# Two-layer trunk of delta-rule and linear-attention heads: another order of the stages, and head outputs read back in parts

## The chip, the cores and the metric

The kernel runs on one core of one Trainium2 chip. The metric is the time of one execution on the device in microseconds (us). Engines are named as in the profile: PE is TensorE, DVE is VectorE, ACT is ScalarE, POOL is GpSimd, SP is SyncE. All DMA transfers of this kernel are issued by SP.

## The reference

One sequence of 2048 tokens with 1024 channels passes two layers. Each layer projects its input to 3608 columns, runs four Gated DeltaNet heads (a short convolution on q, k and v, a delta-rule recurrence over chunks) beside four GLA heads (a gated linear attention over chunks), normalises each head, multiplies it by a SiLU gate, mixes the eight heads with one output projection, and ends with a residual LayerNorm. Everything is float32.

```python
def gated_delta_rule_chunked(q, k, v, g, beta):
    """S_t = a_t (I - b_t k_t k_t^T) S_{t-1} + b_t k_t v_t^T,  o_t = S_t^T q_t."""
    ...
    lower = jnp.eye(c, dtype=f32) + jnp.where(strict, kk * decay, 0.0)
    rhs = jnp.concatenate([vc * bc[..., None], k_beta * jnp.exp(G)[..., None]], axis=-1)
    uw = lax.linalg.triangular_solve(lower, rhs, left_side=True, lower=True)
    ...

def gla_chunked(q, k, v, gk):
    """S_t = diag(exp(gk_t)) S_{t-1} + k_t v_t^T,  o_t = S_t^T q_t."""
    ...

def hybrid_layer(x, w_in, conv_w, ...):
    proj = jnp.einsum("btd,de->bte", x, w_in)
    (dn_q, dn_k, dn_v, dn_z, dn_b, dn_a, g_q, g_k, g_v, g_z, g_r) = _split(proj, IN_SIZES)
    dn_qkv = jax.nn.silu(causal_short_conv(jnp.concatenate([dn_q, dn_k, dn_v], axis=-1), conv_w))
    ...
    o_dn = gated_delta_rule_chunked(q, k, v, g, beta)
    o_dn = head_rms_norm(o_dn, dn_norm_g) * jax.nn.silu(dn_z.reshape(...))
    ...
    o_gla = gla_chunked(gq, gk, gv, log_f)
    o_gla = head_rms_norm(o_gla, gla_norm_g) * jax.nn.silu(g_z.reshape(...))
    o = jnp.concatenate([o_dn.reshape(bsz, t, DN_WIDTH), o_gla.reshape(bsz, t, GLA_WIDTH)], axis=-1)
    y = jnp.einsum("bte,ed->btd", o, w_out)
    return layer_norm(DEEPNORM_ALPHA * x + y, ln_g, ln_b)
```

## The kernel before

**Halves, blocks, chunks.** A layer is computed in two halves of 1024 tokens; the program thus has four halves, and the state of the recurrences is carried from one to the next. A half has two blocks of 512 tokens (b0, b1), and a block has four chunks of 128 (c0 to c7 over the half). Heads 0 to 3 of the output are the delta-rule heads, heads 4 to 7 the GLA heads, which are handled in two pairs (p0, p1).

**Precision.** Matmuls of the projections run in a reduced float32 format; every operand is split in a high part (tiles `wh`, `xt`) and a low part (`wl`, and a second `xt`), and a product takes three matmuls per 128 rows of weights. `load_group` loads 128 columns of the input weights (`wr`) and splits them: a cast to `wh` on ACT, a subtraction to `wl`. `proj_group` multiplies them with a block of the input into a bank `pj` of PSUM: 24 matmuls of 128x512. There are two `pj` banks, three `tr`, two `ch` and one `mg`.

**Stages of a half.** `dense_qk(p)` projects q and k of a GLA pair; `g1(p, b)` is the short-range part of GLA (many matmuls of 128x32 and 64x64), `g2(p, b)` the long-range part, which ends in `finish_head` (four transposes and a copy). `keys(h)`, `values` and `queries` project and convolve a delta-rule head; `dn_decay` spreads its decay factors by way of HBM (`decd`). `dn_invert(h)` inverts the triangular systems of a head, seven steps on DVE, and `dn_merge(h)` joins the inverted blocks with small matmuls in bank `mg`. `gates(e)` projects the gate of head e, multiplies the head's output by it and writes the result, transposed, to HBM: `og[b][e]`.

**The recurrence.** `dn_rec(h, b)` goes through the four chunks of a block. Per chunk it has five matmuls in two `ch` banks: state by keys (its result goes through DVE to `rr`), state by queries (scaled to `qs`), the inverted block by `rr` (scaled on DVE to `vn`), and two products with `vn`, of which one updates the state `Sd` on DVE. Each step waits for the one before: PE, DVE, PE, DVE, PE, DVE.

**Output projection.** `split_o(c, og)` reads the eight gated heads of a chunk back from HBM (512 KB into a tile `m`), casts them to a `wh` tile and subtracts to a `wl` tile. `out_half` multiplies with one half of the columns of the output weights, which `load_wo` has put in `xt` tiles: 16 matmuls with the high part, head by head, then 8 with the low part. `out_proj` runs the 16 pairs of chunk and column half in a fixed sequence, c0, c1 and c2 with the first column half first.

**What sets the order.** No engine gets its instructions as they are written. A `Recorder` notes every operation of the program, with what it reads and writes. `order()` (line 231) then builds the order of each engine by going through a model of time: of the operations whose inputs are done and for whose tile a slot is free (`SLOTS`, `BANKS`), an engine takes the one that was recorded first (`key = program position − lift`), looking at later ones where that one can't start. The durations in it are estimates of the planner. The operations are then issued in this order, each engine in order. So the sequence of the stages in the source is a sequence of priorities, and any change to it can move operations on all engines. Since the recorder's helper issues everything, all lines of the profile read L428, and groups are told apart by tile names.

The stages stand in the source in this sequence (before): dense_qk(0), g1(0,0), values of the second GLA pair, g2(0,0), g1(0,1), dn_decay 0 and 1, dense_qk(1), g2(0,1), dn_decay 2 and 3, g1(1,0), gates 4 and 5, g2(1,0), keys(0), dn_invert(0), g1(1,1), g2(1,1), values and queries of head 0 as one stage (`vq`), dn_merge(0), gates 6 and 7, keys(1); then for each head h the recurrence over both blocks, dn_invert(h+1), vq(h+1), dn_merge(h+1), keys(h+2), and gates(0) after head 2. The gates of heads 1 to 3 follow the recurrence, block 0 first.

## Time and profile before

| | before |
|---|---|
| time, median of 3 runs | 2248.61 us (2245.91 to 2249.0) |
| the profiled execution | 2245.92 us, span 2244.2 us |
| busy PE, DVE, ACT, POOL | 97%, 66%, 49%, 23% of the span |
| DMA | 215.32 MB, 96 GB/s over the span |
| mean granted clock of PE | 0.990 |

PE is the tensor engine's matmuls, PEld its weight loads, which overlap with them. A float32 matmul that isn't in the reduced format shows as two records. Matmul records begin before their forerunner ends, so the time from one start to the next is what one costs. In brackets behind a row of the timeline stands how long the engine sat idle before it, and which engine and tile released it; rows of waits give the total, how often, and the longest. "PEclk" is the share of full clock that PE was granted; in the rows of windows it is the third number from the end.

### The profile page before, as it was taken

The page shows a single profiled execution, that of the slowest core. Times are in us where ns is not written, and L with a number is a line of the kernel's source. Part 1 is how long each engine was busy: PE and PEld are TensorE (multiplying, and loading weights), DVE is VectorE, ACT ScalarE, POOL GpSimd, SP SyncE. Part 2 cuts the span into 40 slices and gives each one's busy share as a digit, 9 for nine tenths or more (in the row PEclk, how much of TensorE's full clock was granted, in tenths as well). Part 3 has the DMA queues.
Part 4 walks back from the last instruction along what each step waited for, and adds up shares of the span by engine and source line. Part 5 has one row for each costly group of instructions (what it writes and reads, how often), then busy time and mean ns, then how long its engine had stood idle before and what let it go on. Part 6 is the DMA issues. An engine that isn't in the chain of part 4 may idle for free.

```text
span 2244.2 us, 44454 instructions
## 1 busy us (share of the span) xinstructions
PE 2165.7 (97%) x16914; PEld 1798.9 (80%) x16914; DVE 1485.1 (66%) x3444; ACT 1098.9 (49%) x3123; POOL 523.8 (23%) x880
## 2 busy tenths in 40 slices
PE   8999999999999999999999999999999999999998
PEld 7877777878887777787888777778788877877877
DVE  3547688756454768875645586887564458688756
ACT  4665455431466545543146654554215665455420
POOL 3333122101143213210122421320011242132001
PEclk9999999999999999999999999999999999999999
DMA  4242222373224131236322323223732232222361
GB/s 139 62 110 64 76 56 58 100 228 123 86 58 123 51 99 45 61 108 215 128 72 71 110 60 92 60 59 106 225 116 69 79 93 66 86 60 69 104 192 57
DMA packets 264542, 215.32 MB, mean 96 GB/s; under 512 B 53060, under 2 KB 211080, under 8 KB 264328
## 3 DMA queue, kind: packets, MB, share of 16 engines
q1 hardware_dynamic: 264328, 212.48, 32.0%
q8 instruction: 133, 2.18, 0.4%
q14 instruction: 81, 0.66, 0.1%
HBM read 166.23 MB, written 46.20 MB: 95 GB/s over the span
## 4 chain that ended last, share of the span: by engine, by line
PE 79%; DVE 10%; DMA 5%; ACT 4%; issue 2%; SPq 0%; POOL 0%; DVEq 0%; ACTq 0%; POOLq 0%
PE pj L428 60%; PE ch L428 9%; PE tr L428 7%; DVE tmp L428 2%; DVE R L428 2%; DMA ud<-Tb 2%; PE mg L428 2%; DVE m L428 2%; ACT m L428 2%; DVE kq L428 1%; DMA U<-ud 1%; DMA m<-nd 1%; DVE Tb L428 1%; ACT wh L428 1%; DMA nd<-T 1%
## 5 line engine op out<-in xcount | busy, mean ns | idle before, releaser
L428 PE MATMUL pj<-xt,wh 128*128 128x512 f32 x4096 | 1102.4, 407 | 18.8 <-ACT wh L428 10.4
L428 PEld LDWEIGHTS pj<-xt,wh 128*128 128x128 f32 x4096 | 748.6, 191 | 167.4 <-ACT wh L428 12.1
L428 PE MATMUL pj<-xt,wl 128*128 128x512 f32 x2048 | 556.6, 401 | 0.0
L428 PEld LDWEIGHTS pj<-xt,wl 128*128 128x128 f32 x2048 | 372.7, 188 | 70.2 <-issue 0.9
L428 POOL TENSOR_TENSOR s<-s,mhalf 128x4 f32<-128x4 f32 (+2 forms) x80 | 94.8, 1185 | 537.2 <-DVE s L428 532.8
L428 POOL TENSOR_TENSOR wl<-wr,wh 128x512 fp32r<-128x512 f32 (+2 forms) x94 | 135.2, 1446 | 308.8 <-ACT wh L428 238.5
L428 PE MATMUL pj<-wh,xt 128*128 128x256 f32 (+1 forms) x1024 | 197.6, 290 | 0.0
L428 DVE TENSOR_TENSOR m<-m,m 128x256 f32<-128x256 f32 (+1 forms) x272 | 132.3, 499 | 55.2 <-ACT m L428 48.8
L428 PEld LDWEIGHTS pj<-wh,xt 128*128 128x128 f32 x1024 | 162.1, 190 | 0.8 <-ACT xt L428 0.4
L428 ACT CAST wh<-wr 128x1024 fp32r<-128x1024 f32 (+2 forms) x116 | 118.2, 1022 | 76.7 <-PE pj L428 57.5
L428 DVE SCALAR_TENSOR_TENSOR kq<-raw,cw,kq 128x512 f32<-128x512 f32 x192 | 152.9, 803 | 3.9
L428 PE MATMUL pj<-wl,xt 128*128 128x280 f32 (+1 forms) x512 | 131.7, 290 | 0.0
L428 DVE TENSOR_TENSOR wl<-wr,wh 128x512 fp32r<-128x512 f32 (+3 forms) x118 | 88.4, 769 | 61.9 <-ACT wh L428 60.9
L428 DVE SCALAR_TENSOR_TENSOR m<-m,pj 128x512 f32<-128x512 f32 x64 | 43.8, 685 | 114.6 <-PE pj L428 114.6
L428 ACT CAST wh<-m 128x1024 fp32r<-128x1024 f32 x32 | 33.1, 1046 | 158.3 <-PE pj L428 158.3
L428 ACT ACTIVATE sq<-m 128x128 bf16<-128x128 f32 x128 | 39.5, 308 | 140.9 <-DVE m L428 132.0
L428 PEld LDWEIGHTS ch<-Sd,kq 128*128 128x128 f32 x512 | 79.9, 192 | 25.6 <-DVE Sd L428 14.2
L428 DVE COPY m<-pj 128x256 f32<-128x256 f32 x18 | 7.6, 423 | 137.0 <-PE pj L428 137.0
L428 PEld LDWEIGHTS pj<-wl,xt 128*128 128x128 f32 x512 | 97.5, 191 | 0.1
L428 PEld LDWEIGHTS ch<-vn,m 128*128 128x128 f32 x512 | 72.8, 192 | 26.9 <-DVE vn L428 17.3
L428 PE MATMUL ch<-Sd,kq 128*128 128x128 f32 x512 | 88.3, 281 | 5.4 <-DVE Sd L428 5.4
L428 PE MATMUL ch<-vn,m 128*128 128x128 f32 x512 | 83.0, 282 | 9.5 <-DVE vn L428 9.5
(192 smaller groups left out, 3420.0 us busy)
## 6 DMA issues: line engine op xcount, KB each, us to landing
wr<-in_w_in_dram SPq DMA_DIRECT2D x104, 512.0 KB, 4.4
m<-decd SPq DMA_DIRECT2D x64, 256.0 KB, 4.3
og<-m SPq DMA_DIRECT2D x64, 256.0 KB, 4.0
m<-in_w_out_dram SPq DMA_DIRECT2D x32, 512.0 KB, 6.0
m<-og SPq DMA_DIRECT2D x32, 512.0 KB, 6.0
m<-in_x_dram SPq DMA_DIRECT2D x16, 512.0 KB, 5.6
m<-gr SPq DMA_DIRECT2D x32, 256.0 KB, 6.1
decd<-m SPq DMA_DIRECT2D x32, 256.0 KB, 2.2
```

Source lines behind the costliest of these rows:

```text
L428: getattr(getattr(self.nc, o.eng), o.name)(*[real(a) for a in o.args], **{k: real(a) for k, a in o.kw.items()})
```

## The change

The sequence of the stages is written as a string, `PLAN`, and differs from the sequence above:

- dense_qk(1) now comes ahead of dense_qk(0);
- g2(p,b) follows its g1(p,b) sooner, and the values of the second GLA pair come after both blocks of the first;
- values and queries of a head are two stages (`v`, `y`), and each block of the recurrence is one (`r` with head and block), with other stages between the two blocks of head 0 (`r00`, `r01`);
- gates 6 and 7 move from ahead of the recurrence to behind the second block of head 0, gates(0) between the queries and the values of head 3.

`split_o` takes a list of parts. For chunks 0, 1 and 2, heads 4 to 7 are read, cast and subtracted first, then heads 0 to 2, then head 3; the other chunks are read whole. `out_half` goes through the heads in the order 4 to 7, 0 to 3. The products and sums are the same; only the order in which the eight heads are summed differs. Per half there are six more DMA transfers, six more casts and six more subtractions.

```diff
--- before.py
+++ after.py
@@ -548,6 +548,10 @@
          "s1": 16, "Sc": 3, "nd": 2, "ud": 2, "og0": 2, "og1": 2, "decd": 2, "bst": 4, "gr": 2, "U32": 1, "T32": 1, "Nd": 2}
 BANKS = {"pj": 2, "tr": 3, "ch": 2, "mg": 1}
 LEVELS_MASK = (16, 8, 4, 2, 1)
+WHOLE, PARTS = ((0, 8),), ((4, 8), (0, 3), (3, 4))
+
+PLAN = ("q1 q0 a00 b00 d1 a01 b01 w d0 a10 g5 b10 g4 a11 k0 v0 d3 i0 b11 m0 y0 r00 k1 d2 y1 "
+        "r01 g6 g7 i1 k2 m1 v1 r10 r11 v2 y2 i2 m2 k3 r20 r21 y3 i3 g0 v3 m3 r30 r31")
 
 
 @with_exitstack
@@ -1248,25 +1252,29 @@
             subtract(lo[:, ks, :], raw, hi[:, ks, :].bitcast(F32))
         return hi, lo
 
-    def split_o(c, og):
+    def split_o(c, og, parts):
 
         b, cs = c // NC, slice((c % NC) * P, (c % NC + 1) * P)
         gl = T([P, KT, P], "m4")
-        nc.sync.dma_start(gl, og[b][:, :, cs].rearrange("h p t -> p h t"))
         oh = T([P, KT, P], "wh", F32R)
         ol = T([P, KT, P], "wl", F32R)
-        nc.scalar.copy(oh, gl)
-        subtract(ol, gl, oh.bitcast(F32))
+        for e0, e1 in parts:
+            es = slice(e0, e1)
+            nc.sync.dma_start(gl[:, es, :], og[b][es, :, cs].rearrange("h p t -> p h t"))
+            nc.scalar.copy(oh[:, es, :], gl[:, es, :])
+            subtract(ol[:, es, :], gl[:, es, :], oh[:, es, :].bitcast(F32))
         return oh, ol
+
+    HEADS = (4, 5, 6, 7, 0, 1, 2, 3)
 
     def out_half(o2, wo, n, y, st):
         (oh, ol), (wh, wl) = o2, wo
         acc = PS([P, BLK], "pj")
-        for k in range(KT):
-            nc.tensor.matmul(acc, oh[:, k, :], wh[:, k, :], start=(k == 0), stop=False)
+        for k in HEADS:
+            nc.tensor.matmul(acc, oh[:, k, :], wh[:, k, :], start=(k == HEADS[0]), stop=False)
             nc.tensor.matmul(acc, oh[:, k, :], wl[:, k, :], start=False, stop=False)
-        for k in range(KT):
-            nc.tensor.matmul(acc, ol[:, k, :], wh[:, k, :], start=False, stop=(k == KT - 1))
+        for k in HEADS:
+            nc.tensor.matmul(acc, ol[:, k, :], wh[:, k, :], start=False, stop=(k == HEADS[-1]))
         nc.vector.scalar_tensor_tensor(out=y, in0=y, scalar=alpha, in1=acc, op0=ALU.mult, op1=ALU.add)
         nc.vector.bn_stats(st[:, n, :], y)
 
@@ -1298,7 +1306,7 @@
                 for i in range(2):
                     nc.sync.dma_start(ys[c][i], src[so + c * P:so + (c + 1) * P, i * BLK:(i + 1) * BLK])
                 if c not in o2:
-                    o2[c] = split_o(c, og)
+                    o2[c] = split_o(c, og, WHOLE)
                 sts[c] = T([P, 2, 6], "bst")
             out_half(o2[c], wo[n], n, ys[c][n], sts[c])
             if n == 1:
@@ -1370,63 +1378,38 @@
                 for b in range(NB):
                     dn_keys(l, h, b, w, xt[b], decd, st)
 
-            def vq(h):
+            def values1():
+                wv1 = load_v(l, 1, False)
+                for b in range(NB):
+                    v[1, b] = proj_v(wv1, xt[b], b, False)
+
+            def rec_block(h, b):
+                oT[h, b] = dn_rec(h, b, dn[h])
+
+            def values(h):
                 w = load_group(l, V0 + P * h)
                 for b in range(NB):
                     dn_values(l, h, b, w, xt[b], dn[h])
+
+            def queries(h):
                 w = load_group(l, Q0 + P * h)
                 for b in range(NB):
                     dn_queries(l, h, b, w, xt[b], decd, dn[h])
 
-            def rec_head(h):
-                for b in range(NB):
-                    oT[h, b] = dn_rec(h, b, dn[h])
-
-            dense_qk(0)
-            g1(0, 0)
-            wv1 = load_v(l, 1, False)
-            for b in range(NB):
-                v[1, b] = proj_v(wv1, xt[b], b, False)
-            g2(0, 0)
-            g1(0, 1)
-            dn_decay(grow, 0, decd)
-            dn_decay(grow, 1, decd)
-            dense_qk(1)
-            g2(0, 1)
-            dn_decay(grow, 2, decd)
-            dn_decay(grow, 3, decd)
-            g1(1, 0)
-            gates(4)
-            gates(5)
-            g2(1, 0)
-            keys(0)
-            dn_invert(dn[0])
-            g1(1, 1)
-            g2(1, 1)
-            vq(0)
-            dn_merge(dn[0])
-            gates(6)
-            gates(7)
-            keys(1)
-            for h in range(4):
-                rec_head(h)
-                if h < 3:
-                    dn_invert(dn[h + 1])
-                    vq(h + 1)
-                    dn_merge(dn[h + 1])
-                if h < 2:
-                    keys(h + 2)
-                if h == 2:
-                    gates(0)
+            stage = {"q": dense_qk, "a": g1, "b": g2, "w": values1, "d": lambda h: dn_decay(grow, h, decd),
+                     "g": gates, "k": keys, "i": lambda h: dn_invert(dn[h]), "v": values, "y": queries,
+                     "m": lambda h: dn_merge(dn[h]), "r": rec_block}
+            for step in PLAN.split():
+                stage[step[0]](*(int(n) for n in step[1:]))
             z = [(e, load_group(l, Z0 + P * e)) for e in (1, 2, 3)]
             for e, w in z:
                 gate(w, xt[0], oT[e, 0], og[0][e])
             wo = [load_wo(l, 0)]
-            o2 = {0: split_o(0, og)}
+            o2 = {0: split_o(0, og, PARTS)}
             for e, w in z:
                 gate(w, xt[1], oT[e, 1], og[1][e])
             for c in (1, 2):
-                o2[c] = split_o(c, og)
+                o2[c] = split_o(c, og, WHOLE if c > 2 else PARTS)
             wo.append(load_wo(l, 1))
             out_proj(l, so, do, src, dst, og, wo, o2)
         cur = nxt
```

What the change moves is shown at three places of the second half of layer 0.

PE at the first recurrence step of head 2 (`ch` with `rr`, `vn`, `Sd`; `mg` is the merge of that head, `tr` and `pj` are queries and keys of head 3 or a gate). Before:

```order
L428 MATMUL pj_146<-xt_115,wl_110 128x512
L428 MATMUL mg_165<-m_6_132,m_13_130 64x64
L428 MATMUL mg_165<-m_16_139,m_13_130 64x64
...
L428 MATMUL ch_149<-rr_203,m_6_132 128x128
L428 MATMUL ch_150<-vn_207,m_1_134 128x128
L428 MATMUL ch_150<-vn_207,m_3_120 128x128
L428 MATMUL ch_149<-Sd_0_92,kq_157 128x128
L428 MATMUL ch_150<-Sd_0_92,kq_161 128x128
L428 MATMUL pj_145<-xt_113,wh_108 128x512
```

And now:

```order
L428 MATMUL mg_165<-m_13_142,m_6_129 64x64
L428 MATMUL pj_145<-xt_114,wh_108 128x512
L428 MATMUL pj_145<-xt_113,wl_111 128x512 x2
L428 MATMUL tr_124<-kq_157,kq_155 128x128 x2
L428 MATMUL ch_150<-rr_203,m_16_143 128x128
L428 MATMUL tr_124<-kq_157,kq_155 128x128 x2
L428 MATMUL tr_122<-ident_63,kq_157 128x128 x2
L428 MATMUL ch_149<-vn_207,m_2_136 128x128
L428 MATMUL ch_149<-vn_207,m_0_117 128x128
L428 MATMUL tr_122<-ident_63,kq_157 128x128 x2
L428 MATMUL pj_145<-xt_113,wl_111 128x512 x2
L428 MATMUL ch_150<-Sd_0_92,kq_162 128x128
```

Between the matmul that takes `rr` and the one that takes `vn` there was nothing; now two products of queries and keys and two transposes stand there, and others behind.

PE at the start of the output projection (`pj` with `xt_114` and `xt_113`, the high and low part of the output weights, and the heads of chunk 0 in `wh_107`, of chunk 1 in `wh_108`). Before, after the last step of the recurrence:

```order
L428 MATMUL pj_146<-xt_115,wl_112 128x512 x3
L428 MATMUL ch_150<-Sd_0_93,kq_162 128x128
L428 MATMUL ch_149<-Sd_0_93,kq_154 128x128
L428 MATMUL ch_150<-rr_204,m_17_141 128x128
L428 MATMUL ch_149<-vn_208,m_11_131 128x128
L428 MATMUL ch_149<-vn_208,m_2_119 128x128
L428 MATMUL pj_145<-xt_114,wh_107 128x512
L428 MATMUL pj_145<-xt_113,wh_107 128x512
```

And now, from the second chunk of that recurrence on (the rows left out are more of the same kinds; the last row is head 3 of chunk 0):

```order
L428 MATMUL ch_149<-ident_63,m_0_126 128x128
L428 MATMUL pj_146<-xt_115,wl_112 128x512 x2
L428 MATMUL pj_145<-xt_114,wh_107 128x512
L428 MATMUL pj_145<-xt_113,wh_107 128x512
L428 MATMUL ch_150<-Sd_0_93,kq_161 128x128
L428 MATMUL ch_149<-Sd_0_93,kq_156 128x128
...
L428 MATMUL ch_149<-vn_208,m_4_140 128x128
L428 MATMUL ch_149<-vn_208,m_2_119 128x128
L428 MATMUL pj_146<-xt_113,wh_108 128x512
L428 MATMUL pj_146<-xt_114,wh_108 128x512
...
L428 MATMUL pj_145<-xt_114,wh_107 128x512
```

The first 14 matmuls of chunk 0 and those of chunk 1 now lie between the steps of the last recurrence, and head 3 of chunk 0 comes behind both.

SP's queue around the last gated head of block 0 (`og_1_100`; it is written by the row with `og_1_100` on the left and 128x512). Before:

```order
L428 DMA og_1_100<-m_18_142 128x512
L428 DMA m_8_133<-in_x_dram 128x512
L428 DMA m_1_134<-in_x_dram 128x512
L428 DMA m_0_117<-og_1_100 128x8x128
L428 DMA m_3_120<-og_1_100 128x8x128
L428 DMA m_4_121<-og_1_100 128x8x128
L428 DMA m_1_118<-in_w_out_dram 128x2x512
```

And now (the first four rows stand 20 rows ahead of the fifth):

```order
L428 DMA m_1_118<-og_1_100 128x4x128
L428 DMA m_1_118<-og_1_100 128x3x128
L428 DMA m_0_117<-og_1_100 128x4x128
L428 DMA m_0_117<-og_1_100 128x3x128
...
L428 DMA og_1_100<-m_12_137 128x512
L428 DMA m_13_142<-in_x_dram 128x512
L428 DMA m_1_118<-og_1_100 128x128
L428 DMA m_0_117<-og_1_100 128x128
L428 DMA m_4_121<-og_1_100 128x128
L428 DMA m_3_120<-in_w_out_dram 128x2x512
```

Seven heads of a chunk are read before the last head is written, and only that head behind it.

## The prediction

> **What bounds the kernel now.** I read the page's busy times first, then the chain that ended last, the busy time by stretch, the waits of TensorE, and last the timeline at each long wait.
>
> ```profile
> PE 2165.7 (97%) x16914; PEld 1798.9 (80%) x16914; DVE 1485.1 (66%) x3444; ACT 1098.9 (49%) x3123; POOL 523.8 (23%) x880
> ...
> PE 79%; DVE 10%; DMA 5%; ACT 4%; issue 2%; SPq 0%; POOL 0%; DVEq 0%; ACTq 0%; POOLq 0%
> ```
>
> TensorE (PE) is busy for 97% of 2244.2 us. The diff adds and removes no matmul, so only three things can move the time: idle time of PE, matmuls that run slowly, and matmuls that cost more for their neighbours. Next the four halves (columns: length, then busy time of PE, its weight loads, VectorE, ScalarE, GpSimd, then the granted clock, DMA share and GB/s):
>
> ```profile
> 0.00:560.00 560.00, 534.33 (x4188) 444.12 (x4189) 366.60 (x855) 276.63 (x785) 137.45 (x262) 0.99 0.35 102
> 560.00:1120.00 560.00, 545.20 (x4262) 452.76 (x4261) 375.80 (x868) 276.32 (x784) 132.36 (x214) 0.99 0.33 97
> 1120.00:1680.00 560.00, 545.71 (x4257) 453.33 (x4255) 371.74 (x863) 277.20 (x784) 129.52 (x205) 0.99 0.33 97
> 1680.00:2244.00 564.00, 540.51 (x4214) 448.64 (x4212) 370.92 (x861) 268.79 (x771) 124.45 (x200) 0.99 0.29 88
> ```
>
> PE idles 14.8 and 14.3 us in the two middle halves, 25.7 in the first and 23.5 in the last. What the outer two have beyond 14.5 belongs to the program's start and end, which the change leaves alone. Some 14.5 x 4 = 58 us are idle time of the order itself. The waits of PE (total us, times, longest):
>
> ```profile
> PE tr L428 <- ACT kq L428: 10.5, 20, 0.7
> PE pj L428 <- ACT wh L428: 10.4, 8, 2.1
> PE ch L428 <- DVE vn L428: 9.5, 8, 2.0
> PE tr L428 <- DMA m<-in_x_dram: 9.2, 1, 9.2
> PE pj L428 <- ACT m L428: 8.4, 8, 1.6
> PE ch L428 <- ACT m L428: 8.2, 12, 0.8
> PE ch L428 <- DVE Sd L428: 5.4, 13, 0.7
> ```
>
> The longest of three rows (2.1, 2.0, 1.6) recur once per half, each at one place of the program; most of the others are below 0.9. The three places, in the first or second half, are these:
>
> ```profile
> 480.49 3.78 PE L428 MATMUL pj<-xt,wh 128*128 128x512 f32 x8 [2.07 <-ACT wh L428]
> ...
> 543.52 3.79 PE L428 MATMUL pj<-xt,wh 128*128 128x512 f32 x16
> ...
> 945.64 0.49 PE L428 MATMUL ch<-rr,m 128*128 128x128 f32 x2 [0.47 <-ACT m L428]
> 948.00 0.71 PE L428 MATMUL ch<-vn,m 128*128 128x128 f32 x4 [1.87 <-DVE vn L428]
> 949.21 0.71 PE L428 MATMUL ch<-Sd,kq 128*128 128x128 f32 x4 [0.50 <-DVE Sd L428]
> ...
> 889.42 0.50 PE L428 MATMUL pj<-xt,wh 128*128 128x512 f32 x1 [1.63 <-ACT m L428]
> ...
> 332.54 0.80 PE L428 MATMUL pj<-xt,wh 128*128 128x512 f32 x1 [1.63 <-ACT m L428]
> ```
>
> The first is the start of the output projection, the second the first recurrence step of head 2, the third a projection for queries of head 2 that wants a bank of PSUM. After the first, eight matmuls take 3.78 us where sixteen of that shape take 3.79 elsewhere (0.23 us each): half speed. The granted clock shows the same (same columns, the clock is the third from the end):
>
> ```profile
> 332.50:335.90 3.40, 3.36 (x10) 2.88 (x11) 2.50 (x6) 2.98 (x8) 1.07 (x1) 0.50 0.02 5
> 393.90:397.30 3.40, 3.01 (x10) 2.73 (x11) 1.94 (x7) 2.08 (x6) 1.37 (x2) 0.50 0.44 73
> 479.20:486.10 6.90, 5.61 (x15) 4.46 (x16) 3.23 (x5) 5.22 (x10) 1.01 (x1) 0.51 1.07 367
> 950.30:953.70 3.40, 3.40 (x12) 2.83 (x11) 2.20 (x4) 0.77 (x3) 0.38 (x2) 0.50 0.87 218
> 1035.60:1039.00 3.40, 3.18 (x8) 2.51 (x9) 2.56 (x3) 3.40 (x7) 0.52 (x1) 0.50 1.05 379
> 1503.20:1506.70 3.50, 3.50 (x13) 2.92 (x12) 2.21 (x5) 1.44 (x5) 0.71 (x2) 0.51 0.65 138
> 1588.60:1595.40 6.80, 5.56 (x15) 4.40 (x16) 3.18 (x5) 5.01 (x9) 1.01 (x1) 0.50 1.07 368
> 2059.60:2063.00 3.40, 3.15 (x10) 2.77 (x11) 1.94 (x6) 1.99 (x6) 1.24 (x2) 0.50 0.49 82
> 2145.00:2151.80 6.80, 5.65 (x15) 4.46 (x16) 3.27 (x5) 5.53 (x10) 1.01 (x1) 0.50 1.07 371
> ```
>
> Nine stretches, 41.0 us, with PE busy 36.4 of them at half clock: 18.2 us lost, of which 10.0 behind the output projection (20.0 us busy), 6.5 behind the recurrence (13.06 busy) and 1.7 behind the bank wait. Each begins near one of the long waits. These gaps of about 2 us thus cost nearly as much again in clock, though the one at 889 us cost none.
>
> [...]
>
> **The change part by part.**
>
> *Output projection (8.3 us of waiting, 10.0 of clock).* The last gated head output of block 0 is written to HBM, and only then is all of chunk 0 read back and cast:
>
> ```profile
> 1025.30 0.33 SPq L428 DMA_DIRECT2D og<-m  x1
> ...
> 1028.34 2.71 SPq L428 DMA_DIRECT2D m<-og  x3
> ...
> 1034.74 1.98 ACT L428 CAST wh<-m 128x1024 fp32r<-128x1024 f32 x2
> ...
> m<-og SPq DMA_DIRECT2D x32, 512.0 KB, 6.0
> ...
> U<-ud SPq DMA_DIRECT2D x16, 128.0 KB, 2.4
> ```
>
> SyncE's queue waits 3.0 us for the write to land, the 512 KB take 6.0, the cast about 1. PE has run out of other work by then. In the change, heads 4 to 7 and 0 to 2 are read before that write, and only 64 KB of head 3 behind it. In the order, 45 of PE's matmuls stand between the last transposes of head 3, block 0 and the first matmul that needs head 3: 30 of 512 columns at 0.23 us and 15 of the recurrence, which at about 0.22 (two records each, four records in 0.61 to 0.71) give 6.9 + 3.3 = 10.2 us. The path beside it: about 2.0 us from those transposes to the write's issue (an estimate from their end at 1023.3 and the issue at 1025.30), 3.0 to landing, 2.4 to 6.0 for 64 KB (no transfer of this size in the trace; the bounds are the 128 KB and 512 KB rows), 0.7 for issue and a small cast: 8.1 to 11.7 us. The wait left is 0 to 1.5 us. I take 0.5 since 64 KB is nearer to 128: gain 4 x 1.57 = 6.3, bounds 2.3 to 8.3. With so short a gap the clock should hold: gain 10, bounds 0 to 10. Of the waits on "wh" 2.1 us (the 10.4 less 8.3) are for weights at the start of the dense stage and stay.
>
> *Recurrence of head 2 (11.4 us of waiting, 6.5 of clock).* The three waits at 945.64 to 949.21 are 2.84 us per half. Ahead of VectorE's vn stand the key operations of head 3:
>
> ```profile
> 944.65 1.13 DVE L428 SCALAR_TENSOR_TENSOR m<-tr,s,m 128x128 f32<-128x128 f32 x4
> ...
> 946.56 1.13 DVE L428 SCALAR_TENSOR_TENSOR m<-tr,s,m 128x128 f32<-128x128 f32 x4
> 947.60 0.34 DVE L428 TENSOR_SCALAR vn<-ch,s 128x128 f32<-128x128 f32 x1
> ...
> L428 DVE SCALAR_TENSOR_TENSOR kq<-raw,cw,kq 128x512 f32<-128x512 f32 x192 | 152.9, 803 | 3.9
> ```
>
> VectorE runs from 944.65 to 947.94 without a pause: it isn't slow, PE is early, because the five recurrence matmuls follow the merge with nothing between. In the changed order two transposes and two products of queries stand between rr and vn, and 19 projection matmuls between the merge's steps. From the last merge copy on VectorE to vn I count four convolution operations (0.80 each), four small ones (0.78, the pause between the two groups above), one group of 1.13 and vn's 0.34: 5.45 us. PE has over the same stretch 19 x 0.23, five at 0.22 and two groups of merge matmuls (below 0.6 each): 6.7 us. That covers vn if VectorE is on time at the copy, but before the copy it carries another 4.5 us of keys and queries against some 3 us on PE (estimates from the same durations). I take a wait of 0.7 left: gain 4 x 2.14 = 8.6, bounds 0 and 11.4; clock 5.5, bounds 0 and 6.5.
>
> *Bank wait in the queries (6.5 us, clock 1.7).* At 889 us the queries of head 2 wait for ScalarE to empty the bank that their values left, and ScalarE is behind with copies for the keys of the same head. In the change the values and queries of head 2 still follow each other, but a merge, the values of head 1 and both of its recurrence blocks stand between the keys of head 2 and them. No row shows the new place. I take 0.4 of 1.63 as left: gain 4.9 and 1.2, bounds 0 and 8.2.
>
> *The other waits.* 58 − 8.3 − 11.4 − 6.5 = 32 us, some 50 waits below 0.9 us. A new order deals them anew: gates 6 and 7 and the split stages put projection matmuls into the recurrence, where VectorE's queue is what PE waits for. Bounds: all gone (32), or 12 us more (the 13.6 us of "ch" waits on ScalarE's m and on Sd nearly double). I take a third as gone: gain 10, which is the weakest term.
>
> *Neighbours.* A stage of small matmuls ends the run of large ones. Sixteen 64x64 matmuls hold PE for 0.61 us:
>
> ```profile
> 886.00 0.68 PE L428 MATMUL mg<-m,m 64*64 64x64 f32 x16
> 886.61 0.96 PE L428 MATMUL pj<-xt,wl 128*128 128x512 f32 x3
> ```
>
> The order has five such excursions fewer per half (41 against 46). One costs between nothing and that whole 0.61; I take 0.2: gain 4, bounds 0 and 12.
>
> *What is added:* per half six transfers, six casts and six subtractions, as three chunks go in three parts. The casts and subtractions have the same elements, and ScalarE (49% busy) and VectorE (66%) are free at that place, since the projection's fill is PE alone; if their queues were full, an added 0.3 us each (the 128-column cast) delays head 3. The transfers stand in SyncE's in-order queue ahead of the second half of the output weights; bounds 0 and 3 us in all, I take 0.
>
> **Sum:** 6.3 + 10 + 8.6 + 5.5 + 4.9 + 1.2 + 10 + 4 = 50.5. The profiled execution took 2245.92 us (span 2244.2), 2.7 below the median of 2248.61. 2245.9 − 50.5 = 2195.4; in the runs' median that is 2195 to 2198, I say 2197. All bounds to the good give 8.3 + 10 + 11.4 + 6.5 + 8.2 + 32 + 12 = 88, 2158; all to the bad 2.3 − 12 − 3, 2259.
>
> **Rivals.**
>
> *Only the tail is cured (2230).* The recurrence and bank waits come back at other heads at equal price. For it: VectorE's queue is as full as before near head 2's merge. Against: the filler between the steps. 6.3 + 10 = 16: 2230.
>
> *Head 3's part is late all the same (2213).* The three small reads follow one another in the same queue, and if each lands as late as a 512 KB read, the projection waits 1.5 us and the clock drops again: the 50.5 lose 6 + 10. Against: 10 us of fill. [...]
>
> *The clock part stays (2214).* If the stretches at half clock don't come from the gaps, 16.7 us of the sum go. For it: the gap at 889 us cost nothing.
>
> *The waits are only dealt anew (2246).* For it: both orders come from the same priorities and the same estimated durations, and each place that waits now was thought covered.
>
> *Slower (2269).* The recurrence is now by block, with the next head's inversion, keys and queries behind it on VectorE. There are 4 x 2 x 4 = 32 block starts; each that waits as head 2's does costs 2.84 + 1.6 of clock. There are four now. With fourteen it is 10 x 4.4 = 44 more, against 16 + 6 kept elsewhere: + 23. It decides from about nine of the 32 on. Against: no run of more than two recurrence matmuls without another stands in the new order.
>
> **How the numbers follow.** Forecast 0.58 (own range 2170 to 2213), tail alone 0.16, late part 0.05, clock 0.05, dealt anew 0.08, slower 0.08. The change takes effect on all engines' orders, so "it does nothing" has no share of its own. About 0.2% (4.5 us) is what a measurement tells from no change. Faster: 0.58 + 0.16 + 0.05 + 0.05 + a fifth of 0.08 = 0.86; slower 0.08; the same 0.06. The range to hold 8 in 10: from 2168 (the lowest tenth of the forecast left out) to 2238 (tail alone, with 8 us to spare).
>
> **What would show it.** Right: PE's idle in the middle halves falls from 14.5 to 5 to 8 us; the row for wh on PE falls from 10.4 to 2 to 4.5; the row for vn falls below 4; the start of the output projection runs at clock 1.0, with 0.23 us per matmul; head 3's part is read in 2 to 4 us. Wrong: new waits on vn or Sd over 1 us in the recurrence, a read of 64 KB that takes 6 us, or stretches at clock 0.5 where no gap stands. The forecast fails if the small waits, of which I follow none singly, grow.

## The result and the profile after

The changed kernel takes 2172.64 us in the median of four runs (2170.08 to 2174.01), the kernel before 2247.26 (four runs). The ratio is 0.967, with a 95% interval of 0.9651 to 0.9689: 74.6 us, or 3.3%, faster. The forecast was 2197, a gain of 50.5.

The page of the profile after, PE's busy time; and the four stretches of its span (columns as before):

```profile
PE 2129.7 (98%) x16914; PEld 1781.7 (82%) x16914; DVE 1527.9 (70%) x3475; ACT 1118.7 (51%) x3126; POOL 520.6 (24%) x910
```

```profile
0.00:543.00 543.00, 527.62 (x4207) 440.88 (x4208) 377.80 (x866) 281.84 (x787) 138.01 (x271) 1.00 0.36 105
543.00:1086.00 543.00, 532.72 (x4239) 446.13 (x4237) 384.00 (x871) 280.77 (x784) 127.82 (x219) 1.00 0.34 99
1086.00:1629.00 543.00, 537.55 (x4259) 449.77 (x4258) 383.73 (x871) 282.60 (x786) 128.53 (x213) 1.00 0.34 101
1629.00:2172.30 543.30, 531.81 (x4215) 444.89 (x4214) 382.39 (x870) 273.49 (x771) 126.20 (x208) 1.00 0.31 91
```

PE executes the same 16914 records. Of the 71.9 us that the span is shorter (2244.2 to 2172.3), 36 are busy time of PE (2165.7 to 2129.7) and 36 idle time. The granted clock is 1.00 in every stretch: in this execution no part of the program but its last microseconds runs at half clock any more. The waits of PE, after:

```profile
PE tr L428 <- DMA m<-in_x_dram: 9.4, 2, 8.9
PE tr L428 <- issue: 6.1, 4, 2.4
PE tr L428 <- ACT kq L428: 3.9, 8, 0.6
PE ch L428 <- DVE vn L428: 3.0, 4, 1.5
PE ch L428 <- DVE m L428: 2.7, 9, 0.6
PE ch L428 <- ACT m L428: 2.4, 4, 1.5
PE pj L428 <- ACT wh L428: 2.1, 4, 0.5
```

The first is the start of the program, as before. The second is three waits of 2.36, 1.89 and 1.65 us and one of 0.2, put down to nothing but "issue", and it is new. They lie in long runs of small matmuls, here in the second half:

```profile
675.16 1.31 PE L428 MATMUL tr<-m,m 128*32 128x32 f32 x120
678.83 0.26 PE L428 MATMUL tr<-m,m 128*32 128x32 f32 x7 [2.36 <-issue]
```

Records that are missing from the trace don't explain them: both kernels have the same 16914. The last section returns to them. The row for vn fell from 9.5 to 3.0, the one for wh from 10.4 to 2.1 (the weights of the dense stage), the one for kq from 10.5 to 3.9; the rows for the bank (8.4) and for Sd (5.4) are gone.

The first recurrence step of head 2, second half, where the matmuls with `rr`, `vn` and `Sd` waited 0.47, 1.87 and 0.50 us, now has the products and transposes of the changed order between them and no wait:

```profile
926.94 0.39 PE L428 MATMUL ch<-rr,m 128*128 128x128 f32 x2
927.17 0.61 PE L428 MATMUL tr<-kq,kq 128*128 128x128 f32 x4
927.61 0.38 PE L428 MATMUL tr<-ident,kq 128*128 128x128 f32 x2
927.83 0.65 PE L428 MATMUL ch<-vn,m 128*128 128x128 f32 x4
```

The start of the output projection, which waited 2.07 us and then ran at half speed, now looks so (PE's timeline, first half; then the transfers):

```profile
465.84 0.94 PE L428 MATMUL pj<-xt,wh 128*128 128x512 f32 x3
466.62 0.68 PE L428 MATMUL ch<-vn,m 128*128 128x128 f32 x4
467.06 1.87 PE L428 MATMUL pj<-xt,wh 128*128 128x512 f32 x7
468.76 1.99 PE L428 MATMUL pj<-xt,wl 128*128 128x512 f32 x8
```

```profile
m<-og SPq DMA_DIRECT2D x20, 512.0 KB, 7.0
m<-og SPq DMA_DIRECT2D x12, 256.0 KB, 4.3
m<-og SPq DMA_DIRECT2D x12, 192.0 KB, 5.0
...
m<-og SPq DMA_DIRECT2D x12, 64.0 KB, 1.9
```

No row waits, and seven matmuls of the output projection take 1.87 us. The read of 64 KB lands in 1.9 us, less than the lower bound of the forecast (2.4); a whole chunk takes 7.0.

**Where the 72 us come from.** I priced each matmul record at its own usual pace (the lower quartile of the time to the next start, for its tile names and shape, where nothing waits; the same prices for both kernels, 1886 us in all). What lies above that price, in us:

| | before | after | difference |
|---|---|---|---|
| idle as the trace shows it (without the wait at the very start) | 61.6 | 26.1 | −35.5 |
| more than the usual pace at those waits, beside the idle time | 19.7 (101 waits) | 11.8 (63) | −7.9 |
| at a change of the tile size from one matmul to the next | 49.9 (422) | 44.8 (378) | −5.1 |
| matmuls in the stretches at half clock, and all others | 209.7 | 186.7 | −23.0 |

Of the last row the stretches at half clock are 20.0 before and nothing after; the other 3 us are small differences among all the rest.

### The profile page after: what moved, and what is told of

The parts are those of the page before. It is cut to its first block, busy times and chain, and to the rows that moved or that the text cites. A ratio compares the mean times of both kernels' runs of the same rounds, so it can differ in the third digit from the quotient of the medians.

```text
span 2172.3 us, 44658 instructions
## 1 busy us (share of the span) xinstructions
PE 2129.7 (98%) x16914; PEld 1781.7 (82%) x16914; DVE 1527.9 (70%) x3475; ACT 1118.7 (51%) x3126; POOL 520.6 (24%) x910
## 4 chain that ended last, share of the span: by engine, by line
PE 58%; DVE 6%; DMA 2%; ACT 2%; issue 1%; POOL 0%; SPq 0%; DVEq 0%; POOLq 0%; ACTq 0%
PE pj L428 44%; PE ch L428 7%; PE tr L428 5%; DVE m L428 2%; DVE R L428 1%; ACT m L428 1%; PE mg L428 1%; DVE tmp L428 1%; DMA ud<-Tb 1%; DMA m<-nd 1%; DVE kq L428 0%; DMA U<-ud 0%; DMA nd<-T 0%; DVE Tb L428 0%; POOL s L428 0%
## 5 line engine op out<-in xcount | busy, mean ns | idle before, releaser
L428 PE MATMUL pj<-xt,wh 128*128 128x512 f32 x4096 | 1080.5, 401 | 2.2 <-ACT wh L428 2.1
L428 PE MATMUL pj<-wh,xt 128*128 128x256 f32 (+1 forms) x1024 | 205.2, 293 | 0.2 <-ACT xt L428 0.2
L428 DVE TENSOR_TENSOR m<-m,m 128x256 f32<-128x256 f32 (+1 forms) x272 | 144.6, 547 | 30.7 <-ACT m L428 21.8
L428 POOL TENSOR_TENSOR wl<-wr,wh 128x512 fp32r<-128x512 f32 (+1 forms) x77 | 106.1, 1387 | 246.5 <-ACT wh L428 129.7
L428 DVE SCALAR_TENSOR_TENSOR kq<-raw,cw,kq 128x512 f32<-128x512 f32 x192 | 144.5, 760 | 5.4 <-ACT kq L428 2.3
L428 DVE TENSOR_TENSOR wl<-wr,wh 128x512 fp32r<-128x512 f32 (+1 forms) x135 | 99.2, 759 | 45.5 <-ACT wh L428 40.4
L428 ACT CAST wh<-m 128x1024 fp32r<-128x1024 f32 (+3 forms) x56 | 37.1, 680 | 137.4 <-PE pj L428 137.2
L428 POOL MEMSET m<- 128x512 f32 (+1 forms) x160 | 79.1, 509 | 95.1 <-PE tr L428 84.3
L428 PEld LDWEIGHTS ch<-Sd,kq 128*128 128x128 f32 x512 | 76.7, 190 | 19.7 <-DVE Sd L428 11.3
```

The source lines that it names most:

```text
L428: getattr(getattr(self.nc, o.eng), o.name)(*[real(a) for a in o.args], **{k: real(a) for k, a in o.kw.items()})
```

## The experiments

The old sequence of stages, written as a plan string, gives the very program of the kernel before, so parts of the change can be set one by one. Where chunks are read whole, the heads are multiplied in the order 0 to 7, as before. All times are medians; the runs were taken in three groups, each with its own runs of the kernel before (2246.37, 2244.91 and 2245.74 us), to which the ratios refer.

| run | what | us | ratio to before (95%) |
|---|---|---|---|
| e1_plan_whole | new sequence, chunks read whole | 2219.15 | 0.9863 to 0.9895 |
| e2_parts_only | old sequence, chunks in parts | 2224.51 | 0.9885 to 0.9922 |
| e3_front | new front, old recurrence part, whole | 2250.0 | 1.001 to 1.0034 |
| e4_back | old front, new recurrence part, whole | 2264.17 | 1.0058 to 1.0098 |
| e5_fill | before, with idle work in the gap | 2236.35 | 0.9949 to 0.9976 |
| e6_gates | changed, gates 6 and 7 as before | 2230.08 | 0.9916 to 0.9957 |
| e7_gate0 | as e1, gate of head 0 later | 2216.88 | 0.985 to 0.9902 |
| e8_heads | changed, heads in the order 0 to 7 | 2196.03 | 0.9767 to 0.9807 |
| e9_queries | changed, queries of head 1 later | 2192.41 | 0.9748 to 0.9787 |
| e10_blocks | changed, first recurrence block later | 2178.85 | 0.9687 to 0.9721 |
| e11_dense | changed, dense stages in the old order | 2172.74 | 0.9654 to 0.9695 |
| e12_oldgates | before, gates 6 and 7 later | 2238.06 | 0.996 to 0.9984 |

### The sequence without the parts, and the parts without the sequence

```diff
-WHOLE, PARTS = ((0, 8),), ((4, 8), (0, 3), (3, 4))
+WHOLE, PARTS = ((0, 8),), ((0, 8),)
...
-    HEADS = (4, 5, 6, 7, 0, 1, 2, 3)
+    HEADS = (0, 1, 2, 3, 4, 5, 6, 7)
```

> The changed sequence of stages, but every chunk read back whole and the heads multiplied in the order 0 to 7. Theory (the split alone mends the start of the output projection): the waits on the cast return there, 4 x 2.07 us, with the half-speed stretch behind them (10 to 12 us in all), so about 2172.6 + 20 = 2193 us, and the row of PE waiting for ACT's wh grows from 2.1 to 10 us. Rival (the new sequence alone puts enough work there): 2172 to 2176 us, the row stays near 2.

e2 keeps the parts and the order of heads, and has the old plan:

```diff
-PLAN = ("q1 q0 a00 b00 d1 a01 b01 w d0 a10 g5 b10 g4 a11 k0 v0 d3 i0 b11 m0 y0 r00 k1 d2 y1 "
-        "r01 g6 g7 i1 k2 m1 v1 r10 r11 v2 y2 i2 m2 k3 r20 r21 y3 i3 g0 v3 m3 r30 r31")
+PLAN = ("q0 a00 w b00 a01 d0 d1 q1 b01 d2 d3 a10 g4 g5 b10 k0 i0 a11 b11 v0 y0 m0 g6 g7 k1 "
+        "r00 r01 i1 v1 y1 m1 k2 r10 r11 i2 v2 y2 m2 k3 r20 r21 i3 v3 y3 m3 g0 r30 r31")
```

> The sequence of stages of before, with chunks 0 to 2 read back in three parts and the heads multiplied in the order 4 to 7, 0 to 3. Theory (the two parts of the change add): 8 us of waits and 10 to 12 us of half speed go, 2247 - 20 = 2227 us. Rival (head 3's part lands too late without the new sequence): a wait of 1 to 2 us stays at head 3, the half-speed stretch stays, 2240 to 2247 us.

e2 came as expected: 22 us faster than before. e1 did not: the parts are worth 46.5 us in the new sequence (2219.15 against 2172.64), more than twice what they are worth in the old one and what I gave them. PE's timeline of e1, first half, at the last recurrence and the start of the output projection:

```profile
456.84 0.71 PE L428 MATMUL ch<-Sd,kq 128*128 128x128 f32 x4 [0.32 <-ACT m L428]
...
458.86 0.68 PE L428 MATMUL ch<-vn,m 128*128 128x128 f32 x4 [0.54 <-DVE vn L428]
459.98 1.22 PE L428 MATMUL ch<-Sd,kq 128*128 128x128 f32 x4 [0.44 <-DVE Sd L428]
...
462.55 1.19 PE L428 MATMUL ch<-vn,m 128*128 128x128 f32 x4 [0.54 <-DVE vn L428]
464.18 1.22 PE L428 MATMUL ch<-Sd,kq 128*128 128x128 f32 x4 [0.44 <-DVE Sd L428]
...
466.75 1.19 PE L428 MATMUL ch<-vn,m 128*128 128x128 f32 x4 [0.54 <-DVE vn L428]
469.94 1.65 PE L428 MATMUL pj<-xt,wh 128*128 128x512 f32 x3 [2.00 <-ACT wh L428]
```

The wait of 2.00 us is back, as expected. But the last three chunks of the recurrence stand bare: the new sequence has spent the gate of head 0 earlier, and the heads' gates of block 1 are used up at 456.0. The steps that use `vn` and `Sd` then wait 0.32 to 0.54 us each, and from 459.8 on the clock is at half (a row of 128x128 records takes 1.2 us in place of 0.7). With the parts, 28 matmuls of chunks 0 and 1 are free to stand between these steps. So the parts do two things: they take away the wait for the read, and they are filler for the last recurrence. In the old sequence (e2), where most of the last recurrence has other filler, they are worth 22 us; the other half of the 46.5 us is thus put down to the filler, and the forecast had these matmuls only as cover for the read.

The same accounting as above for e1 against the changed kernel: idle 44.7 against 26.1, beside the waits 16.5 against 11.8, the stretches at half clock and all others 210.3 against 186.7, changes of tile 43.4 against 44.8. At least half of the 46 us is clock: the matmuls in e1's stretches at half clock alone are 23.0 above their price (mean granted clock 0.986 in e1, 0.999 in the changed kernel).

### Filler for the last recurrence: the order of heads, and the gate of head 0

```diff
-    HEADS = (4, 5, 6, 7, 0, 1, 2, 3)
+    HEADS = (0, 1, 2, 3, 4, 5, 6, 7)
```

> The changed kernel, with the heads multiplied in the order 0 to 7; the reads stay in three parts. Only six matmuls of chunks 0 and 1 each can start before head 3 is there, and two chunks of the last recurrence stand bare. Theory (the 28 matmuls that the parts free are filler for the recurrence): waits of 0.3 to 0.6 us at each bare step and a stretch at clock 0.5, 2172.6 + 4 x 6 = 2197 us. Rival (the parts help because the wait for the read goes, and the order of heads is nothing): 2172 to 2178 us.

2196.03 us, as the theory said. Here only six matmuls of each chunk come before head 3, twelve in place of 28. PE's timeline of e8, first half:

```profile
462.66 0.68 PE L428 MATMUL ch<-vn,m 128*128 128x128 f32 x4 [0.54 <-DVE vn L428]
...
465.74 0.68 PE L428 MATMUL ch<-vn,m 128*128 128x128 f32 x4 [0.54 <-DVE vn L428]
467.68 3.91 PE L428 MATMUL pj<-xt,wh 128*128 128x512 f32 x9 [1.26 <-ACT wh L428]
```

The reads are split as in the change; still the last steps are bare, head 3 is waited for by 1.26 us, and nine matmuls take 3.91 us, 0.43 each in place of 0.23. Without the order of the heads, half of what the split gains (23 of 46.5 us) is lost.

```diff
-        "r01 g6 g7 i1 k2 m1 v1 r10 r11 v2 y2 i2 m2 k3 r20 r21 y3 i3 g0 v3 m3 r30 r31")
+        "r01 g6 g7 i1 k2 m1 v1 r10 r11 v2 y2 i2 m2 k3 r20 r21 y3 i3 v3 m3 g0 r30 r31")
```

> The changed sequence, chunks read whole, heads 0 to 7, and the gate of head 0 moved from ahead of the values of head 3 to behind its merge. Theory (what the read whole costs in the changed sequence, 2219 against 2173 us, is the last recurrence running without filler at half speed): 48 matmuls of the gate fill part of it, two bare chunks stay instead of two and a half, the stretch at clock 0.5 shortens, 2205 to 2215 us. Rival (the cost is the late read alone): 2217 to 2221 us.

2216.88 us lies between the two ranges, 0.1 us below the rival's, and 2 us from e1. In the trace the planner spent the gate's matmuls ahead of the last chunks all the same; two chunks and one step stay bare, against three chunks, and the mean granted clock is 0.988 against 0.986. The edit hardly moved what it was to move, so the run decides nothing; e8 is the test that counts.

### Does the half clock come from the gap?

Added in the kernel before, ahead of the output projection:

```diff
+            fill = PS([P, P], "mg")
+            for _ in range(6):
+                nc.tensor.matmul(fill, Sd[3], ident, start=True, stop=True)
             out_proj(l, so, do, src, dst, og, wo, o2)
```

> The kernel before with six matmuls of 128x128 more per half (the last state of head 3 by the identity, into a free bank, read by nobody), which stand between the last recurrence step and the output projection and add work but take nothing away. Theory (the half speed behind a gap comes from PE's inactivity): the gap of 2.07 us shrinks to below 0.7, the stretches at clock 0.5 behind the output projection's start go, and the added work makes the kernel faster: 2246.4 - 10 = 2236 us. Rival (the stretches come anyway): 2246 to 2248 us, the clock there stays 0.5.

2236.35 against 2244.91 us: work that nobody reads made the kernel 8.6 us faster. PE's timeline of e5, second half:

```profile
1031.07 0.71 PE L428 MATMUL ch<-vn,m 128*128 128x128 f32 x4 [0.45 <-DVE vn L428]
1032.23 1.60 PE L428 MATMUL mg<-ident,Sd 128*128 128x128 f32 x12 [0.44 <-DVE Sd L428]
1033.85 2.12 PE L428 MATMUL pj<-xt,wh 128*128 128x512 f32 x8
```

The projection starts when it would have started anyway, and its eight matmuls take 2.12 us in place of 3.58 to 3.78. The mean granted clock of the profiled execution is 0.994 in place of 0.990. This shows the clock as a cost of its own beside the wait, and the sign and rough size of the forecast's 10 us for it at this place.

### The stages one by one

e3 and e4 cut the plan behind the queries and the merge of head 0 and join the front of one sequence to the rest of the other:

```diff
 # e3: new front, old rest (e4: old front, new rest)
+PLAN = ("q1 q0 a00 b00 d1 a01 b01 w d0 a10 g5 b10 g4 a11 k0 v0 d3 i0 b11 m0 y0 d2 g6 g7 k1 "
+        "r00 r01 i1 v1 y1 m1 k2 r10 r11 i2 v2 y2 m2 k3 r20 r21 i3 v3 y3 m3 g0 r30 r31")
+PLAN = ("q0 a00 w b00 a01 d0 d1 q1 b01 d2 d3 a10 g4 g5 b10 k0 i0 a11 b11 v0 y0 m0 r00 k1 y1 "
+        "r01 g6 g7 i1 k2 m1 v1 r10 r11 v2 y2 i2 m2 k3 r20 r21 y3 i3 g0 v3 m3 r30 r31")
```

> The changed sequence up to the merge of head 0 (GLA stages, keys, values and queries of head 0), the old one from there on, chunks read whole. Theory (most of the gain comes from the recurrence stages behind): PE's idle time falls by no more than 5 us and the neighbours of small matmuls give 5 us, 2247 - 8 = 2239 us. Rival (the front carries half of it): 2220 us or less.

> The old sequence up to the merge of head 0, the changed one from there on, chunks read whole. Theory: the waits on vn, the bank wait in the queries and the half-speed stretch at the recurrence of head 2 go, with most of the small waits; 2247 - 42 = 2205 us, and the only stretches at half speed are those at the output projection. Rival (the gain needs the front too): 2225 us or more.

Both theories were wrong, and on the same side (e4 lies in its rival's range): neither half of the sequence gains anything without the other, e3 is 0.2% and e4 0.8% slower than before. e4 has the bare last recurrence of e1, and both have a long wait, four times, that neither whole sequence has. In e3 and in e4 it is, in the second half:

```profile
934.88 2.08 PE L428 MATMUL tr<-kq,kq 128*128 128x128 f32 x8 [6.03 <-ACT kq L428]
```

```profile
793.09 0.66 PE L428 MATMUL tr<-ident,m 128*128 128x128 f32 x4 [4.54 <-ACT m L428]
```

The next run shows what such a wait is made of.

```diff
-PLAN = ("... i0 b11 m0 y0 r00 k1 d2 y1 r01 g6 g7 i1 k2 ...")
+PLAN = ("... i0 b11 m0 y0 g6 g7 r00 k1 d2 y1 r01 i1 k2 ...")
```

> The changed kernel with the gates 6 and 7 back ahead of the recurrence, all else as changed. Theory (projection work kept for the recurrence is what hides its steps): head 0's or 1's recurrence gets waits on vn, Sd or the merge, 8 us of idle or more in all and perhaps new stretches at half speed, 2172.6 + 12 = 2185 us (2178 to 2195). Rival (their place doesn't matter): 2170 to 2176 us.

2230.08 us: the theory's sign, at five times its size (57 us), and beyond its range. By the accounting above, 39 of the 57 us are idle time and 16 the stretches at half clock (mean granted clock 0.992 against 0.999). The waits come at two places, four times each: 4.99 us, shown here, and 2.70 us, shown in the last section. PE's, then DVE's, then ACT's rows in the second half:

```profile
866.96 1.98 PE L428 MATMUL pj<-xt,wl 128*128 128x512 f32 x8
873.92 1.11 PE L428 MATMUL tr<-ident,kq 128*128 128x128 f32 x4 [4.99 <-ACT kq L428]
```

```profile
866.39 1.09 DVE L428 TENSOR_TENSOR tmp<-Tb,m 128x896 f32<-128x896 f32 x1
867.51 1.09 DVE L428 TENSOR_REDUCE R<-tmp 128x32 f32<-128x896 f32 x1
...
870.89 2.32 DVE L428 SCALAR_TENSOR_TENSOR kq<-raw,cw,kq 128x512 f32<-128x512 f32 x3
```

```profile
873.24 0.63 ACT L428 ACTIVATE kq<-kq 128x512 f32<-128x512 f32 x1 [1.02 <-DVE kq L428]
```

While DVE inverts the systems of head 1 (`tmp`, `R`, `Tb`), the convolution of the keys of head 2 (`kq`) stands behind it in DVE's queue. PE has projected these keys and has nothing else: the gates 6 and 7, whose 96 matmuls at 0.23 us are 22 us of work, stood here in the changed kernel. DVE is busy for 69% of e6's span, but through this stage it has no pause; the waits of e3 and e4 stand behind the last inversion steps in the same way. The forecast's rival "slower" had PE waiting for this full queue, but at the starts of the recurrence's blocks; the wait found here is at the keys of the next head. The changed sequence keeps clear of it.

```diff
-PLAN = ("... r00 k1 d2 y1 r01 g6 g7 i1 k2 m1 v1 r10 ...")
+PLAN = ("... r00 k1 d2 r01 g6 g7 i1 k2 m1 v1 y1 r10 ...")
```

> The changed kernel with one stage moved: the queries of head 1 behind its values (as before) in place of ahead of the second recurrence block of head 0. Theory (each stage of projections covers the convolution chain on ACT and DVE of the stage before it, and the recurrence steps beside it): the keys of head 1 or the recurrence lose that cover, PE waits 10 us or more in all, 2185 to 2200 us. Rival (the place of this stage is free): 2170 to 2177 us.

2192.41 us: 20 us slower than the change, in the theory's range; 11 us are idle time and 9 the stretches at half clock (mean granted clock 0.994 against 0.999). But the wait is not where the theory had it, at the keys or in the recurrence: it is in a merge, 2.2 us in each half, and the profile puts it down to DVE:

```profile
305.14 0.22 PE L428 MATMUL mg<-U,Y 32*32 32x32 f32 x2 [2.23 <-DVE Y L428]
```

```diff
-PLAN = ("... m0 y0 r00 k1 d2 y1 r01 g6 g7 ...")
+PLAN = ("... m0 y0 k1 d2 y1 r00 r01 g6 g7 ...")
```

> The changed kernel with the first recurrence block of head 0 moved behind the keys and queries of head 1, so that its two blocks follow each other as before. Theory (what matters is that projections stand between the steps; the gates 6 and 7 are there for both blocks): 2172 to 2182 us. Rival (splitting the recurrence into blocks is what gains): 2190 us or more.

2178.85 us, in the theory's range, 6 us slower than the change: splitting the recurrence of head 0 by block is a small part.

```diff
-PLAN = ("q1 q0 a00 b00 ...")
+PLAN = ("q0 q1 a00 b00 ...")
```

> The changed kernel with the two dense GLA stages in the old order, the first pair ahead of the second. Theory (this part of the change is a detail): 2169 to 2177 us. Rival (the first pair's gates must wait for it): 2185 us or more.

2172.74 us: the order of the dense stages makes no difference that can be measured.

```diff
-PLAN = ("... v0 y0 m0 g6 g7 k1 r00 r01 i1 v1 ...")
+PLAN = ("... v0 y0 m0 k1 r00 r01 g6 g7 i1 v1 ...")
```

> The kernel before with one stage moved: the gates 6 and 7 from ahead of the keys of head 1 to behind the recurrence of head 0, chunks read whole. Theory (a stage is worth what it covers in its own neighbourhood, so a move that is worth 57 us in the new sequence is worth nothing by itself): 2240 to 2270 us. Rival (these gates in the recurrence are the gain): 2215 us or less.

2238.06 us, 8 us faster than before and 2 below the theory's range. The long waits at the recurrence of head 2 and at the bank are gone, and waits of 4.5 and 1.7 us per half on a convolution (`kq`) have come, of the kind of e6's. A stage whose place is worth 57 us in one sequence is worth 8 in the other. No run beats the changed kernel; e11 equals it. What the new order of the other GLA stages is worth inside the new sequence was not tested by itself.

## Why the prediction was right, and where its sizes were off

The time of 2172.64 us lies in the stated range of 2168 to 2238, 4.6 us from its lower end; the gain has the forecast sign, and the sum had two thirds of it: 50.5 of 74.6 us.

**What bounds the kernel.** PE's order, as stated: the same records, and the whole gain is idle time, clock, and what matmuls cost beside waits and at their neighbours.

**The output projection.** The path was right: head 3's part lands before it is needed, no wait is left, and the clock stays at 1.00. The rivals of a late part and of a clock that falls anyway are out: the 64 KB take 1.9 us, and in e5, with the gap filled, eight matmuls take 2.12 us in place of 3.58 to 3.78. What was mis-sized is the worth of the term, 6.3 + 10 = 16.3 us. In the old sequence it measures 22 (e2); in the new one 46.5 (e1), since the last recurrence would be bare without it. I saw the 28 matmuls in the order and counted them as time that hides the read, not as time that hides the steps of the recurrence. The prediction's own rows for a bare recurrence, at 945.64 to 949.21, had the price.

**The recurrence of head 2, and the bank wait.** Both are gone whole (2.84 and 1.63 us per half, with their clock) where I left 0.7 and 0.4. Gain at the two places 11.4 + 6.5 in place of 8.6 + 4.9.

**The other waits.** 35 us of idle time in the same accounting before, 26 after: 9 against the 10 of the forecast. That the weakest term held is luck in part: the waits of the old kinds fell by 15, and 6.1 us put down to "issue" came new, of which the sum had nothing. (The small waits before were nearly 70 by the page's rows of waits, not some 50.)

**The clock.** 20 us against 16.7 (18.2 lost in all by the prediction's reckoning): I left residues where none stayed, and the matmuls in those stretches lie somewhat further above their price than half of the busy time.

**Neighbours.** 5.1 against 4.

**What the sum left out.** 7.9 us beside the waits. A wait shows as idle only from the modelled end of the matmul before it; its first part, on average 0.19 us (19.7 us over 101 waits, 11.8 over 63), lies under that matmul's own duration. By that mean a wait of 0.5 us costs nearly 0.7 (an estimate). Together, by the rows of the table: 35.5 + 7.9 + 5.1 + 23.0 = 71.5 against 50.5.

**The parts as a sum.** The forecast added two independent gains, 16 for the parts and 34 for the sequence. The runs don't add: the sequence alone gives 27 us, the parts alone 22, both 74.6. Added up they would give 49, close to the 50.5 of the forecast; nearly the whole miss, some 25 us, is what the two parts give only together, and the sum had no term for that. That 49 is near 50.5 is luck: the sequence alone gave less than its 34, the parts more than their 16. The rivals by mechanism: "only the tail" is out (e1, e2); "slower" is out for the change itself, but PE out of work while DVE's queue is full is the larger part of e6's 57 us, and with the bare last recurrence it makes e4 slower than before; e4 doesn't separate the two.

**What the profile was to show.** The row for wh fell to 2.1 and the one for vn to 3.0, as stated. PE's idle time in the two middle halves is 10.3 and 5.5 us, where 5 to 8 was stated; the first holds waits of 1.2 and 1.5 us that came new with the sequence, at a merge and at the first recurrence step of head 1, and two of those put down to "issue". A wait on vn of over 1 us in the recurrence, stated as a sign of being wrong, thus did come, in one half of the four; it is small beside what went.

## What to carry to other kernels

Ask of every stage of dense matmuls which chain on the other engines runs beside it, and price a move by what then stands bare: at the place it leaves, too. Work that a change frees earlier is worth what it covers, which can be more than the wait that the change was looked at for; and two parts of a change that share the same filler don't add. Here a wait cost its idle time, on average 0.19 us more that the trace shows as busy, and at nine places of the kernel before a stretch at half clock of 3.4 to 6.9 us.

## What the runs showed of the hardware

**The half clock followed some gaps and not others of the same length.** In the kernel before, PE has twelve gaps of over 1.6 us behind the start of the program. At all four of 2.06 to 2.07 us (output projection) and all four of 1.87 to 2.00 us (recurrence of head 2) the clock fell to 0.50 for 3.4 to 6.9 us, before the gap had ended or within 2.3 us of its end; of the four of 1.63 and 1.64 us (the bank), at one. In the 3.4 us ahead of these nine stretches PE was busy for 1.04 to 1.96 us. The kernel before, around the gaps that end at 332.54 and at 889.42:

```profile
329.10:332.50 3.40, 1.81 (x22) 1.41 (x21) 3.14 (x15) 2.75 (x10) 1.81 (x2) 1.00 0.15 54
885.40:888.80 3.40, 2.40 (x28) 1.88 (x26) 3.04 (x16) 2.73 (x13) 2.02 (x2) 1.00 0.28 77
888.80:892.20 3.40, 2.78 (x16) 2.52 (x17) 3.19 (x9) 3.34 (x8) 0.48 (x1) 1.00 0.01 2
```

In the first row PE is busy for 1.81 us of 3.4, and the clock is 0.50 from 332.5 to 335.9; the second gap is shared by rows with 2.40 and 2.78 us, and the clock stays at 1.00. The busy time does not tell the cases apart either: at the gaps that end at 1443.12 and 1999.19, PE is busy for 1.77 us of 1441.40 to 1444.80 and 1.76 us of 1997.40 to 2000.80, and the 3.4 us behind each are at 1.00. What decides between the four gaps of 1.63 and 1.64 us was not shown. In e6 a gap of 2.70 us leaves 0.70 us busy in one row, and another time is shared by two, of which the second is still at 1.00:

```profile
381.20:384.60 3.40, 0.70 (x6) 0.57 (x6) 3.30 (x6) 1.79 (x3) 1.43 (x3) 1.00 0.05 11
934.20:937.60 3.40, 1.90 (x9) 1.24 (x7) 3.26 (x6) 1.74 (x2) 1.27 (x1) 1.00 0.00 0
937.60:941.00 3.40, 2.20 (x16) 2.08 (x17) 3.33 (x6) 1.52 (x5) 1.05 (x3) 1.00 0.13 39
```

In e1 the clock fell without a long gap. Waits of at most 0.54 us with short matmuls between them leave PE busy for 2.00 of 3.4 us, and the next three rows are at 0.50:

```profile
456.40:459.80 3.40, 2.00 (x11) 1.34 (x10) 1.95 (x6) 1.53 (x5) 0.00 (x0) 1.00 0.68 208
459.80:463.20 3.40, 2.67 (x9) 2.11 (x10) 1.02 (x4) 0.77 (x3) 0.00 (x0) 0.50 0.68 202
463.20:466.70 3.50, 2.56 (x9) 1.67 (x8) 1.25 (x4) 0.77 (x3) 0.00 (x0) 0.50 1.20 277
466.70:470.10 3.40, 1.35 (x5) 1.08 (x5) 0.88 (x4) 1.33 (x3) 0.87 (x1) 0.50 0.93 335
```

**The last small read landed early.** In the changed kernel the reads of 64 KB landed in 1.9 us in the median, those of 192 KB in 5.0, of 256 KB in 4.3, all for chunks 0 to 2; whole reads of 512 KB, for the later chunks, took 7.0. Other transfers were under way (in the first half DMA share 0.32 from 463 to 467 us and 0.96 from 467 to 471), so these times are not the price of a read by itself.

**Waits for "issue" in long runs of small matmuls.** The new front of the sequence puts 192 small matmuls (tile 128*32) in a row, where the old one has 128 at most. In the changed kernel three waits of 2.36, 1.89 and 1.65 us put down to "issue" lie in such runs, at three of the twelve. Each of them ends 1.3 to 1.4 us after a 16 KB transfer of the queue that the page calls instruction (q8) has ended, and there are only 133 such transfers in 2172 us; what holds PE there was not shown. All nine kernels with the new front (after, e1, e3, e6 to e11) have a row for "issue" of 5.3 to 6.4 us, three or four waits with the longest of 1.8 to 2.4 us; the kernel before has none, and among the longest rows of the other four with the old front there is none. Behind the three waits of the changed kernel the clock stays at 1.00. They are 6 us that the change costs, and that another order of the front might save; this was not tried.
